# A decoder layer on one core: the heads' gate is projected ahead of the values, the values are turned round later, two exponentials are joined, and the first products of a block inverse run over 64 columns

## The chip, the core and the metric

The kernel runs on one core of a Trainium2 chip. The core has a matrix engine (TensorE, in the profile PE, with its weight loads in rows of their own, PEld), a vector engine (VectorE, DVE), an engine for activation functions (ScalarE, ACT), a general one (GpSimd, POOL) and one that here only starts transfers (SyncE, SP). The metric is the time of one execution on the device, in microseconds (us); the time before is the median of three runs, 2674.58 us.

## The reference, cut to what matters

One layer: a projection of 2048 tokens feeds four heads of a gated delta rule and four heads of HGRN2; their outputs go through an output projection, then come an MLP and a gated embedding. The change lies in the delta rule's heads (and one constant of the output projection's stage). Per head, with chunks of tokens:

```python
qkv = jax.nn.silu(causal_depthwise_conv(qkv, gdn_conv))      # four taps along time
q, k = l2norm(q), l2norm(k)
beta = jax.nn.sigmoid(b_gdn)
g    = -jnp.exp(a_log) * jax.nn.softplus(a_gdn + dt_bias)
gc   = jnp.cumsum(g, axis=-1)                                # inside a chunk
decay = jnp.exp(where(causal, gc[..., :, None] - gc[..., None, :], -inf))
lmat = einsum('bhncd,bhnsd->bhncs', k * beta[..., None], k) * decay
a_mat = eye(c) + where(strict, lmat, 0.0)                    # unit lower triangle
u = solve(a_mat, v * beta[..., None])
w = solve(a_mat, k * beta[..., None] * jnp.exp(gc)[..., None])
k_tail = k * jnp.exp(gc[..., -1:] - gc)[..., None]
# per chunk: v_new = u - w s ;  o = (q exp(gc)) s + qk v_new ;  s = s * exp(gc_last) + k_tail' v_new
o = gated_head_norm(o, gdn_norm, z_gdn)                      # rms norm, then times silu(z)
```

All of it is float32, with a tolerance that the kernel keeps by splitting the operands of its large products into two parts of a shorter float format.

## The kernel before, in words

**Stages.** The program runs through (1) the first embedding tiles, (2) the mixers: the input projection and the eight heads, one quarter `q` of 512 tokens after the other, (3) the output projection, (4) the MLP, (5) the gate of the embedding. The change touches stage 2, and one table of stage 3.

**The clock of stage 2.** For a quarter, `works` holds one small projection (`ab`, the decays) and then, for each of four head pairs `h`, eight projections of 128 channels in the order of `KINDS`: keys `k`, queries `q`, values `v`, the delta head's gate `z`, and HGRN2's `f`, `i`, query and gate. Their tiles are called `mm_4_q_h` (keys), `mm_0` (queries), `mm_8` (values), `mm_12` (the gate z), `mm_16`, `mm_20`, `mm_24`, `mm_28`. Each is 24 matmuls of 128 x 512 (three terms for each of eight slices of the model width) in three steps of eight; after each step a clock ticks (`tick`). A work's result is drained by its function (`to_k`, `to_z` and so on) after its third step. The PSUM banks of these projections come from a pool of two (`pm`), so that a projection cannot start before the one two places ahead has been drained. The first quarter also splits each weight tile on ACT and DVE (L172, L173) and stores the pair; the other quarters load the stored pair.

**A conv and a gate.** `conv_silu` (L557 on) drains a projection with one ACT copy (L560) and three DVE operations that read the bank (L564), one tick later comes the SiLU on ACT. A gate (`gate`, L597) is a single SiLU on ACT (L599).

**A delta head.** `gdn_mixer` is a generator; each of its steps is put into an agenda at a tick (`A_STEPS`, `A_FIRST` for the first head, `A_LAST` for the last, the first two steps of later heads by `A_AHEAD`). Counted from the start of its head's eight projections: the decays' exponentials (L637 to L647) at tick -6, the keys turned (`t_kg`) at 7, the products `kk` of keys with keys and queries at 10, the values turned (`t_vg`, L692, evacuated by four ACT copies into `vt`) and the triangle stored to DRAM (`ud`, L700) at 12, the triangle's 32 x 32 blocks solved by substitution on DVE (L719 to L735) at 16 to 23, the blocks joined to 64 and then to 128 by matmuls (`psp5`, `psx5`, `pst5`, then `psp6`, `psd6`, all by `pairs`, L753) at 30 to 36, and the four chunks' recurrence (`psa`, `psb`, `psc`) at 38 to 53. A head starts every 24 ticks, so the joining of one head's blocks lies beside the next head's keys, queries and values. The small matmuls are in float32 and use one pool of four banks (`pp`) in turn.

**What sets the order.** On PE and SP the instructions stand as the program writes them. On ACT and DVE a scheduler sets the order at build time. An engine runs its own queue strictly in order. An activation function that is not among those loaded is preceded by a load of a function table (`ACT_TABLE_LOAD`).

**Stage 3.** The output projection's tiles are computed in an order written out in `OUT_ORDER`; the norm of quarter 1's rows (`normed`) runs in steps at the ticks of `OUT_LAST` after its last tile: the sum of squares is split (`hl_o`), and at the second entry two matmuls with ones (`nrm_o`, L1197 and L1198) spread it.

## Time and profile before

| | |
|---|---|
| three runs | 2675.51, 2670.68, 2674.58 us |
| the profiled execution | 2671.73 us, of it 2669.9 us from the first instruction to the last |
| PE, PEld busy | 2639.4 us (99%), 2210.5 us (83%) |
| DVE, ACT, POOL busy | 1963.1 us (74%), 1491.8 us (56%), 136.4 us (5%) |
| granted clock of PE | 0.999 |
| transfers | 573.51 MB, 64% of the 16 engines' time on the main queue |

In the rows, a line number with a name is an operation's place in the kernel and the tile that it writes, with buffer numbers left out; `out<-in`, the shape, a count, and after the bar the busy time, the mean duration in ns and the idle time before it with what ended it. A float32 matmul of the program is two MATMUL records and two LDWEIGHTS records in the trace, a transpose one of each.

### The profile page before, as it was taken

To read this page: it belongs to the slowest core of one execution; us is meant where nothing else is said; L and a number is where in the kernel's file an instruction comes from. 1 tells how busy PE (TensorE), PEld (TensorE's weight loads), DVE (VectorE), ACT (ScalarE), POOL (GpSimd) and SP (SyncE) were. 2 spreads that over 40 slices of the span, in tenths; PEclk is the share of its full clock that TensorE was granted. 3 is DMA by queue.
4 is the path that set the end of the run, shared out by engine and by line. 5 is a ranking of instruction groups with operands and counts; after the bars stand their busy time and mean duration, and the time that the engine had idled before them with its cause. 6 is when DMAs were issued, how large, how long until landed. Compare 5 with 4: busy or idle time off the path is not lost. (4 is left out here: it accounts for less than half of the span.)

```text
span 2669.9 us, 38295 instructions
## 1 busy us (share of the span) xinstructions
PE 2639.4 (99%) x12745; PEld 2210.5 (83%) x12745; DVE 1963.1 (74%) x4016; ACT 1491.8 (56%) x3025; POOL 136.4 (5%) x147
## 2 busy tenths in 40 slices
PE   8899999999999999999999999999999999999999
PEld 6788888888888888878888888888888888888887
DVE  7677767777677677578988867767877765468776
ACT  7776655466546556566556555555555555565422
POOL 0000000000000000010000000001000001101000
PEclk9999999999999999999999999999999999999999
DMA  8777777667666665683665576666544465687663
GB/s 279 278 239 248 246 252 248 230 230 252 218 208 224 226 218 187 197 248 107 222 219 198 175 243 218 208 208 214 197 170 144 164 230 190 195 254 251 207 220 131
DMA packets 267766, 573.51 MB, mean 215 GB/s; under 512 B 55578, under 2 KB 60152, under 8 KB 250416
## 3 DMA queue, kind: packets, MB, share of 16 engines
q1 hardware_dynamic: 265264, 566.86, 64.0%
q0 software_dynamic: 2304, 4.20, 0.9%
q8 instruction: 101, 1.65, 0.3%
q14 instruction: 97, 0.79, 0.1%
HBM read 410.57 MB, written 160.37 MB: 214 GB/s over the span
## 5 line engine op out<-in xcount | busy, mean ns | idle before, releaser
L1134 PE MATMUL mm<-xt,w 128*128 128x512 f32 x3072 | 783.8, 400 | 5.4 <-DVE acc_vg L564 3.1
L1134 PEld LDWEIGHTS mm<-xt,w 128*128 128x128 f32 x3072 | 553.1, 189 | 106.4 <-issue 3.7
L1166 PE MATMUL d<-db,da 128*128 128x512 f32 x2688 | 612.8, 389 | 0.0
L1166 PE MATMUL u<-t,wu 128*128 128x512 f32 x2604 | 591.8, 389 | 0.1
L1166 PEld LDWEIGHTS d<-db,da 128*128 128x128 f32 x2688 | 504.5, 188 | 104.8
L1166 PEld LDWEIGHTS u<-t,wu 128*128 128x128 f32 x2604 | 488.6, 188 | 102.3 <-ACT wu L172 0.5
L226 DVE TENSOR_TENSOR db<-db 128x512 fp32r<-128x512 f32 x224 | 159.5, 712 | 59.5 <-ACT db L225 59.1
L1564 DVE TENSOR_TENSOR u<-u,u 128x512 f32<-128x512 f32 x224 | 150.4, 682 | 53.5 <-PE u L1166 52.0
L225 ACT ACTIVATE db<-db 128x512 fp32r<-128x512 f32 x224 | 140.9, 629 | 63.9 <-DMA db<-hid 61.4
L1166 PE MATMUL mmg<-h2T,wg 128*128 128x512 f32 (+1 forms) x792 | 174.7, 383 | 0.0
L1166 PEld LDWEIGHTS mmg<-h2T,wg 128*128 128x128 f32 x792 | 145.5, 188 | 29.1
L1607 ACT ACTIVATE u<-u 128x512 f32<-128x512 f32 x128 | 80.7, 630 | 154.2 <-DVE u L1564 153.8
L173 DVE TENSOR_TENSOR da<-da 128x512 fp32r<-128x512 f32 x128 | 94.2, 736 | 92.1 <-ACT da L172 91.7
L172 ACT ACTIVATE da<-da 128x512 fp32r<-128x512 f32 x128 | 80.6, 630 | 128.1 <-DMA da<-sumd 109.0
L1166 PE MATMUL mmo<-mixT,w_out 128*128 128x512 f32 x600 | 137.9, 390 | 1.7 <-DVE w_out L173 1.0
L1166 PEld LDWEIGHTS mmo<-mixT,w_out 128*128 128x128 f32 x600 | 112.4, 188 | 26.2 <-DVE w_out L173 1.9
L172 ACT ACTIVATE wu<-a 128x512 fp32r<-128x512 f32 x124 | 75.1, 623 | 53.0 <-DMA a<-in_w_up_dram 50.7
L173 DVE TENSOR_TENSOR wu<-a,wu 128x512 fp32r<-128x512 f32 x124 | 86.0, 695 | 8.8 <-ACT wu L172 8.3
L173 DVE TENSOR_TENSOR da<-dr,da 128x512 fp32r<-128x512 f32 x96 | 68.3, 711 | 25.6 <-ACT da L172 24.4
L1608 ACT ACTIVATE u<-u 128x512 f32<-128x512 f32 x128 | 80.4, 628 | 3.0
L172 ACT ACTIVATE da<-dr 128x512 fp32r<-128x512 f32 x96 | 60.5, 630 | 34.0 <-DMA dr<-in_w_down_dram 26.8
L242 POOL TENSOR_TENSOR acc_y<-acc_y,sq_y 128x512 f32<-128x512 f32 x28 | 38.1, 1359 | 757.7 <-ACT sq_y L241 757.7
(393 smaller groups left out, 3838.9 us busy)
## 6 DMA issues: line engine op xcount, KB each, us to landing
w<-cache_in SPq DMA_DIRECT2D x96, 1024.0 KB
db<-hid SPq DMA_DIRECT2D x224, 256.0 KB
cache_in<-w SPq DMA_DIRECT2D x32, 1024.0 KB
hid<-u SPq DMA_DIRECT2D x128, 256.0 KB
da<-sumd SPq DMA_DIRECT2D x128, 256.0 KB
a<-in_w_up_dram SPq DMA_DIRECT2D x124, 256.0 KB
hid<-ht SPq DMA_DIRECT2D x96, 256.0 KB
dr<-in_w_down_dram SPq DMA_DIRECT2D x96, 256.0 KB
```

The costliest lines, as they stand in the source:

```text
L172: S.activation(t[:, 0], raw, AF.Copy)
L173: eng.tensor_tensor(t[:, 1], raw, t[:, 0], ALU.subtract)
L225: S.activation(t[:, 0], plain(t), AF.Copy)
L226: V.tensor_tensor(t[:, 1], plain(t), t[:, 0], ALU.subtract)
L242: eng.tensor_tensor(acc, acc, sq, ALU.add)
L1134: PE.matmul(ps, *terms[i], start=i == 0, stop=i == nt - 1)
L1166: PE.matmul(ps, a, b, start=start, stop=stop)
L1564: V.tensor_tensor(c[new], c[old], ps, ALU.add)
L1607: S.activation(c[k], c[k], AF.Relu)
L1608: S.activation(c[k], c[k], AF.Square)
```

## The change

- `KINDS` projects the gate z third and the values fourth.
- The values' transposes and their four ACT copies move from the step at tick 12 into the first step of the substitution, at tick 16.
- `exp(gc)` (`eg`) was an ACT operation of its own into a tile `cc`; now DVE copies `gc` beside the tail's argument, and one ACT exponential takes both (128 x 8 for two of 128 x 4).
- `gb`, the tile of the decays' sums, is one tile zeroed once; before, each quarter zeroed it.
- The first joining of blocks multiplies only the 64 of 128 columns that are read afterwards: the right-hand operands of `psp5`, `psx5` and `pst5` are 64 columns wide, their left-hand operands stay 128 wide.
- `OUT_LAST` puts all steps after the first one tick later.

```diff
@@ -48,7 +48,7 @@
 SHARE = 6
 TOGETHER = ((1, 7), (1, 6))
 OUT_STEPS = (1, 5) + tuple(range(7, 20)) + (29, 31)
-OUT_LAST = (1, 4) + tuple(range(5, 18)) + (19, 23)
+OUT_LAST = (1, 5) + tuple(range(6, 19)) + (20, 24)
 MLP_STEPS = (1, 7) + tuple(range(9, 27, 2))
 AMID_STEPS = (1, 7) + tuple(range(12, 39, 3))
 
@@ -512,13 +512,14 @@
 
             return ready
 
+        gb = mt("gb", "gb", 1, (36, QT))
+        V.memset(gb, 0.0)
+
         def decays(ps, q):
 
-            gb = mt(f"gb_{q}", "gb", 1, (36, QT))
             sp = m2.tile([4, QT], F32, tag="tmp", name=f"sp_{q}")
             se = m2.tile([4, QT], F32, tag="th", name=f"se_{q}")
             S.activation(sp, ps[0:4, :], AF.Identity, bias=dec[:, 1:2])
-            V.memset(gb, 0.0)
             S.activation(gb[32:36, :], ps[32:36, :], AF.Tanh, scale=0.5)
             V.tensor_scalar(gb[32:36, :], gb[32:36, :], 0.5, 0.5, ALU.mult, ALU.add)
             V.scalar_tensor_tensor(se, sp, -1.0, sp, ALU.mult, ALU.max)
@@ -632,14 +633,14 @@
             gc = gcol[:, :, h : h + 1].rearrange("p c o -> p (c o)")
             beta = gcol[:, :, 32 + h : 33 + h].rearrange("p c o -> p (c o)")
             cd = sm.tile([P, NC], F32, tag="cd", name=f"cd_{n}")
-            tail = sm.tile([P, NC], F32, tag="tail", name=f"tail_{n}")
+            both = sm.tile([P, 2, NC], F32, tag="tail", name=f"tail_{n}")
+            tail, eg = both[:, 0], both[:, 1]
             glast = gf[:, :, P - 1]
             S.activation(cd, glast, AF.Exp)
             V.tensor_tensor(tail, glast, gc, ALU.subtract)
-            S.activation(tail, tail, AF.Exp)
-            both_cc = sm.tile([P, 2, NC], F32, tag="cc", name=f"cc_{n}")
-            eg, ncc = both_cc[:, 0], both_cc[:, 1]
-            S.activation(eg, gc, AF.Exp)
+            V.tensor_copy(eg, gc)
+            S.activation(both, both, AF.Exp)
+            ncc = sm.tile([P, NC], F32, tag="cc", name=f"cc_{n}")
             e = mt(f"e_{n}", "e")
             V.tensor_tensor(by_pair(e), by_pair(gf), negm[:, None].broadcast_to([P, NC // 2, 2, P]), ALU.add)
             for c in range(NC):
@@ -689,11 +690,6 @@
             V.tensor_tensor(qT, qT, flat(gf), ALU.mult)
             qg = qT
             yield
-            psv = turned(live.pop("v"), f"v{n}", pp)
-            vt = mt(f"vt_{n}", "vt", 2)
-            for c in range(NC):
-                S.activation(vt[:, c, :], psv[:, blk(c)], AF.Copy, scale=inv[:, c : c + 1])
-
             ud = dr.tile([NC, NB, SB, SB], F32, name=f"ud_{n}")
             for b in range(NB):
                 sl = slice(b * SB, (b + 1) * SB)
@@ -727,6 +723,10 @@
                 t = fix[:, :, :width]
                 V.tensor_tensor(t, below[:, part_m, part_i], next_to[:, part_m].broadcast_to([P, SB // 4, width]), ALU.mult)
                 V.tensor_tensor(above[:, part_m, part_i], above[:, part_m, part_i], t, ALU.add)
+            psv = turned(live.pop("v"), f"v{n}", pp)
+            vt = mt(f"vt_{n}", "vt", 2)
+            for c in range(NC):
+                S.activation(vt[:, c, :], psv[:, blk(c)], AF.Copy, scale=inv[:, c : c + 1])
             for i in range(0, SB, 2):
                 j = SB - 2 - i
                 if i:
@@ -760,20 +760,25 @@
 
 
 
-            psp = pair_bank("psp5")
-            pairs(psp, um[5], two(xn))
+            def ends(t):
+                return bass.AP(t.tensor, t.offset, [list(t.ap[0]), [P, 2], [3 * SB, 2], [1, SB]])
+
+            def half_bank(name):
+                return bank(f"{name}_{n}", pp)[:, : QT // 4].rearrange("p (a i) -> p a i", a=2)
+
+            psp = half_bank("psp5")
+            pairs(psp, um[5], ends(xn))
             for g in range(NB):
-                S.activation(part[5][rows_of(g), :, rows_of(g ^ 1)], psp[rows_of(g), :, rows_of(0 if g % 2 else 3)],
+                S.activation(part[5][rows_of(g), :, rows_of(g ^ 1)], psp[rows_of(g), :, rows_of(0 if g % 2 else 1)],
                              AF.Copy)
             yield
-            psx, pst = pair_bank("psx5"), pair_bank("pst5")
-            pairs(psx, two(xt), part[5])
-            pairs(pst, part[5], two(xt))
+            psx, pst = half_bank("psx5"), half_bank("pst5")
+            pairs(psx, two(xt), ends(part[5]))
+            pairs(pst, part[5], two(xt)[:, :, SB : 3 * SB])
             for g, to in ((1, 0), (2, 1)):
-                V.tensor_copy(by_pair(xn)[rows_of(g), :, g // 2, rows_of(to)], psx[rows_of(g), :, rows_of(3 * to)])
+                V.tensor_copy(by_pair(xn)[rows_of(g), :, g // 2, rows_of(to)], psx[rows_of(g), :, rows_of(to)])
             for g in range(NB):
-                at_b = rows_of(1 + g % 2)
-                S.activation(two(xt)[rows_of(g), :, at_b], pst[rows_of(g), :, at_b], AF.Copy)
+                S.activation(two(xt)[rows_of(g), :, rows_of(1 + g % 2)], pst[rows_of(g), :, rows_of(g % 2)], AF.Copy)
             yield
             psp = pair_bank("psp6")
             pairs(psp, um[6], two(xn))
@@ -964,7 +969,7 @@
         def to_hg(ps, q, h, g, b):
             b["z"] = gate(ps, f"gh{q}_{h}")
 
-        KINDS = ((4, to_k), (0, to_q), (8, to_v), (12, to_z), (16, to_f), (20, to_i), (24, to_hq), (28, to_hg))
+        KINDS = ((4, to_k), (0, to_q), (12, to_z), (8, to_v), (16, to_f), (20, to_i), (24, to_hq), (28, to_hg))
         decay = {}
         works = []```

**Where instructions stand, first place.** On DVE in the first quarter's first head: the products `kk` are multiplied by the decays (`u`, `qk`, `y_qg`), weights are split (`w_20`), and the values' taps `acc_vg` drain the bank of `mm_8`. Before:

```order
L685 TENSOR_SCALAR u_g0_0_898<-kk_g0_0_0_900,cc_g0_0_816,e_g0_0_818 128x128 x2
L688 TENSOR_TENSOR qk_g0_0_899<-kk_g0_0_0_900,e_g0_0_818 128x256
L564 TENSOR_SCALAR acc_vg0_0_860<-mm_8_0_0_784,cols_87,acc_vg0_0_860 128x509
L685 TENSOR_SCALAR u_g0_0_898<-kk_g0_0_2_908,cc_g0_0_816,e_g0_0_818 128x128
L564 TENSOR_SCALAR acc_vg0_0_860<-mm_8_0_0_784,cols_87,acc_vg0_0_860 128x510
L685 TENSOR_SCALAR u_g0_0_898<-kk_g0_0_2_908,cc_g0_0_816,e_g0_0_818 128x128
L564 TENSOR_SCALAR acc_vg0_0_860<-mm_8_0_0_784,cols_87,acc_vg0_0_860 128x511
L173 TENSOR_TENSOR w_20_0_0_868<-raw_20_0_0_780,w_20_0_0_868 128x1024
```

The same place after:

```order
L686 TENSOR_SCALAR u_g0_0_892<-kk_g0_0_0_894,cc_g0_0_817,e_g0_0_818 128x128 x2
L689 TENSOR_TENSOR qk_g0_0_893<-kk_g0_0_0_894,e_g0_0_818 128x256
L686 TENSOR_SCALAR u_g0_0_892<-kk_g0_0_2_902,cc_g0_0_817,e_g0_0_818 128x128 x2
L689 TENSOR_TENSOR qk_g0_0_893<-kk_g0_0_2_902,e_g0_0_818 128x256
L173 TENSOR_TENSOR w_20_0_0_862<-raw_20_0_0_780,w_20_0_0_862 128x1024
L690 TENSOR_TENSOR y_qg0_0_776<-y_qg0_0_776,gf_g0_0_737 128x512
L565 TENSOR_SCALAR acc_vg0_0_919<-mm_8_0_0_869,cols_87,acc_vg0_0_919 128x509
L565 TENSOR_SCALAR acc_vg0_0_919<-mm_8_0_0_869,cols_87,acc_vg0_0_919 128x510
L565 TENSOR_SCALAR acc_vg0_0_919<-mm_8_0_0_869,cols_87,acc_vg0_0_919 128x511
```

The values' taps stood between the operations on `kk`, and stand now behind all of them and behind a weight split.

**Second place.** On ACT at the end of the same head: `qk_h0_0` are the two halves of HGRN2's query SiLU that drain `mm_24`, `w_4_0_1` is the next head's first weight split, `cd`, `tail`, `e` and `gf` are the next head's decays. Before:

```order
L829 ACT_TABLE_LOAD
L829 ACTIVATE qk_h0_0_988<-mm_24_0_0_1052 128x256
L172 ACTIVATE w_4_0_1_1045<-raw_4_0_1_994 128x1024
L637 ACT_TABLE_LOAD
L637 ACTIVATE cd_g0_1_1065<-gf_g0_1_1028 128x4
L639 ACTIVATE tail_g0_1_1066<-tail_g0_1_1066 128x4
L646 ACTIVATE e_g0_1_1072<-e_g0_1_1072,gcol_0_800 128x128 x4
L647 ACTIVATE gf_g0_1_1028<-gf_g0_1_1028 128x512
L829 ACT_TABLE_LOAD
L829 ACTIVATE qk_h0_0_988<-mm_24_0_0_1052 128x256
```

After:

```order
L834 ACTIVATE iT_h0_0_1042<-mm_20_0_0_988 128x256 x2
L834 ACTIVATE qk_h0_0_978<-mm_24_0_0_1052 128x256 x2
L855 ACTIVATE hb_h0_0_1177<-qk_h0_0_978 128x256
L862 ACTIVATE hb_h0_0_1177<-qk_h0_0_978 128x256
L172 ACTIVATE w_4_0_1_1045<-raw_4_0_1_984 128x1024
L639 ACT_TABLE_LOAD
L639 ACTIVATE cd_g0_1_1065<-gf_g0_1_1028 128x4
L642 ACTIVATE tail_g0_1_1066<-tail_g0_1_1066 128x8
L647 ACTIVATE e_g0_1_1072<-e_g0_1_1072,gcol_0_800 128x128 x4
L648 ACTIVATE gf_g0_1_1028<-gf_g0_1_1028 128x512
```

The two halves now stand together, ahead of the decays and with one table load fewer; the next weight split stands behind two copies `hb` that need DVE's work on `qk_h`. Over the whole program ACT has 86 table loads before and 68 after.

**Third place.** On ACT in the second head, where the first head's blocks are joined: `part5` copies `psp5` and is read by `psx5` and `pst5`, `xt_g0_0` evacuates `pst5`, the `xs1` are sums of squares of the next quarter's input. Before:

```order
L660 ACTIVATE kt_g0_1_1324<-t_kg0_1_1319,tail_g0_1_1066 128x128 x4
L494 ACTIVATE xs1_0_1_1271,ss2_x1_1233<-xs1_0_1_1271 128x512
L766 ACTIVATE part5_577<-psp5_g0_0_1349 32x2x32 x4
L560 ACTIVATE acc_vg0_1_1369<-mm_8_0_1_1289,cols_87 128x512
L561 ACTIVATE hist_572<-mm_8_0_1_1289 128x3
L889 ACTIVATE keys_h0_0_4_1424<-qk_h0_0_988 128x2x4x32
L674 ACTIVATE q2_g0_1_1430<-y_qg0_1_1281 128x512
L172 ACTIVATE w_20_0_1_1377<-raw_20_0_1_1285 128x1024
L494 ACTIVATE xs1_1_0_1337,ss2_x1_1233<-xs1_1_0_1337 128x512
L776 ACTIVATE xt_g0_0_1201<-pst5_g0_0_1409 32x2x32 x4
```

After:

```order
L661 ACTIVATE kt_g0_1_1324<-t_kg0_1_1319,tail_g0_1_1066 128x128 x4
L574 ACTIVATE y_qg0_1_1281<-acc_qg0_1_1274 128x512
L772 ACTIVATE part5_577<-psp5_g0_0_1349 32x2x32 x4
L600 ACTIVATE zt_zg0_1_1369<-mm_12_0_1_1289 128x512
L894 ACTIVATE keys_h0_0_4_1418<-qk_h0_0_978 128x2x4x32
L675 ACTIVATE q2_g0_1_1424<-y_qg0_1_1281 128x512
L172 ACTIVATE w_16_0_1_1282<-raw_16_0_1_1220 128x1024
L494 ACTIVATE xs1_0_0_1234,ss2_x1_1233<-xs1_0_0_1234 128x512
L494 ACTIVATE xs1_0_1_1271,ss2_x1_1233<-xs1_0_1_1271 128x512
L781 ACTIVATE xt_g0_0_1201<-pst5_g0_0_1403 32x2x32 x4
```

The squares and a weight split moved from ahead of `part5` to between `part5` and `xt_g0_0`.

## The prediction

> **What bounds the kernel now.** I read the page first, then busy time by stretches (start and end, length, then busy time with counts of PE, PEld, DVE, ACT and POOL, PE's granted clock, the transfers' share), then PE's own waits (in all, times, longest).
>
> ```profile
> span 2669.9 us, 38295 instructions
> PE 2639.4 (99%) x12745; PEld 2210.5 (83%) x12745; DVE 1963.1 (74%) x4016; ACT 1491.8 (56%) x3025; POOL 136.4 (5%) x147
> 60.00:400.00 340.00, 331.81 (x1795) 282.51 (x1794) 252.35 (x690) 222.32 (x553) 17.84 (x21) 1.00 0.75 251
> 400.00:700.00 300.00, 299.20 (x1660) 257.84 (x1659) 222.88 (x650) 174.57 (x458) 19.41 (x22) 1.00 0.69 234
> 700.00:1060.00 360.00, 358.81 (x1987) 308.61 (x1986) 259.53 (x757) 197.36 (x513) 18.06 (x21) 1.00 0.68 218
> 1060.00:1250.00 190.00, 185.50 (x864) 153.72 (x863) 136.41 (x220) 115.65 (x200) 17.69 (x19) 1.00 0.65 197
> ```
>
> PE is the bound, at a granted clock of 1.00. It idles 30.5 us in all. In the stretches with the mixers (60 to 1060 us) it idles 8.2, 0.8 and 1.2 us, and 4.5 us in the one with the output projection. So the change can pay in two ways only: less work on PE, or fewer of these 14.7 us. What is saved on ACT or DVE alone is worth nothing where no row below waits for it.
>
> ```profile
> PE mm L1134 <- DVE acc_vg L564: 3.1, 1, 3.1
> PE nrm_o L1197 <- ACT hl_o L172: 2.6, 1, 2.6
> PE kk_g L681 <- ACT xt_g L776: 1.4, 1, 1.4
> PE mm L1134 <- ACT qk_h L829: 1.3, 1, 1.3
> PE kk_g L682 <- ACT y_qg L573: 0.7, 2, 0.4
> PE psx_g L753 <- ACT part L766: 0.7, 1, 0.7
> ```
>
> Five of the six lie in the first two heads, at 68 to 128 us. Each has a row in the steps below.
>
> **The 64 columns (PE work): taken as 0.** 16 heads x 6 matmuls (two each of `psp5`, `psx5`, `pst5`) x 2 records = 192 records get half the columns.
>
> ```profile
> 1062.02 0.60 PE L753 MATMUL psx_g<-part,xt_g 128*128 128x128 f32 x4
> 1062.46 0.61 PE L753 MATMUL pst_g<-xt_g,part 128*128 128x128 f32 x4
> L753 PEld LDWEIGHTS psx_g<-part,xt_g 128*128 128x128 f32 x64 | 9.6, 190 | 2.5 <-ACT part L766 1.1
> L594 PEld LDWEIGHTS t_vg<-cst,y_vg 128*128 128x128 f32 x64 | 7.6, 141 | 0.6
> 812.17 0.14 PEld L541 LDWEIGHTS ps_gb<-cst,gbb 36*128 36x128 f32 x1
> 812.24 0.14 PEld L541 LDWEIGHTS ps_gb<-cst,gb 36*128 36x128 f32 x1
> 812.48 0.30 PEld L1134 LDWEIGHTS mm<-xt,w 128*128 128x128 f32 x2
> ```
>
> Four records take 0.44 us from one start to the next group's, 0.11 us each. Is this the streaming of columns or the load of weights, which each record has? The last row is a pair of loads on an idle array, 0.30 us long with 0.19 for one: the second starts 0.11 us after the first, before the first matmul of 512 columns can have streamed. So a load of the 190-ns kind by itself holds the next one off for 0.11 us, what a record costs now. Loads for transposes are shorter (141 ns) and come 0.07 us apart with 36 columns behind them, so these rows don't bound ours from below. The weights stay 128 wide, so half the columns leave the 0.11 us. Bounds: nothing, or half of 192 x 0.11 = -10.6 us if streaming alone counts. I take nothing, since the load row is of the very shape. The Trainium skill ("TensorE: Matmul & The Clock Gate", Back-to-back issue gap) has the isolated gap go with the number of columns; by that rule the sum would get the full -10.6 us, a rival below. The same page's section on LDWEIGHTS gives 128 columns / 1.2, that is 107 ns, whatever the matmul behind it streams; by that the sum gets 0, and the 0.11 us of the pair of loads agrees.
>
> **The gate ahead of the values, first head: -2.7 us.** Before, three convolutions in a row need DVE, and the third shares it with `kk`.
>
> ```profile
> 71.99 0.61 DVE L685 SCALAR_TENSOR_TENSOR u_g<-kk_g,cc_g,e_g 128x128 f32<-128x128 f32 x2
> 72.52 0.41 DVE L688 TENSOR_TENSOR qk_g<-kk_g,e_g 128x256 f32<-128x256 f32 x1
> 73.39 1.04 ACT L172 ACTIVATE w<-raw 128x1024 fp32r<-128x1024 f32 x1
> 74.67 0.74 DVE L564 SCALAR_TENSOR_TENSOR acc_vg<-mm,cols,acc_vg 128x511 f32<-128x511 f32 x1
> 75.33 1.22 DVE L173 TENSOR_TENSOR w<-raw,w 128x1024 fp32r<-128x1024 f32 x1
> 75.56 2.06 PE L1134 MATMUL mm<-xt,w 128*128 128x512 f32 x8 [3.10 <-DVE acc_vg L564]
> 77.82 18.43 PE L1134 MATMUL mm<-xt,w 128*128 128x512 f32 x80
> ```
>
> PE could have gone on at 72.46 (75.56 less 3.10). After the change the bank that it needs then is the gate's, drained by one ACT operation; the values' bank is needed one projection later: 24 matmuls at 18.43/80 = 0.23 us, so at 72.46 + 5.5 = 78.0. On DVE (first order excerpt) come first four `u` and two `qk`, from 71.99 on 2 x 0.61 + 2 x 0.41 = 2.0, then the split (1.22, behind ACT's at about 73.2), `y_qg` (0.7, from the same timeline) and three taps (3 x 0.74): 71.99 + 2.0 + 1.2 + 0.7 + 2.2 = 78.1, with hand-overs 78.4. What is late next is this same bank, by 0.4. In later heads the same sum has no weight split, and about 1 us to spare.
>
> **Two halves of a SiLU together: -0.4 us.** Before, the second half stands behind the next head's decays and two table loads; after, it doesn't.
>
> ```profile
> 92.66 0.38 ACT L829 ACTIVATE qk_h<-mm 128x256 f32<-128x256 f32 x1 [3.48 <-PE mm L1134]
> 99.81 1.43 PE L1134 MATMUL mm<-xt,w 128*128 128x512 f32 x5 [1.27 <-ACT qk_h L829]
> 104.26 0.43 DVE L855 TENSOR_TENSOR qk_h<-qk_h,gg_h 128x256 f32<-128x256 f32 x1
> ```
>
> That wait (1.27) goes, but the second order excerpt puts the next weight split behind `hb`, which needs four DVE operations of 0.43 between pieces of the substitution. From the end of `mm_24`: two halves 0.7, DVE 4 x 0.43 + 0.75, `hb` 0.43, split 1.04 on ACT, decays' two DVE operations 0.85, split 1.22: 6.7 us, against 24 matmuls and four transposes on PE, 5.9. A wait of 0.8 to 0.9 takes its place.
>
> **The second head: -1.8 us.**
>
> ```profile
> 119.64 1.06 ACT L172 ACTIVATE w<-raw 128x1024 fp32r<-128x1024 f32 x1 [0.18 <-DMA cache_in<-w]
> 120.89 0.63 ACT L494 ACTIVATE xs<-xs 128x512 f32<-128x512 f32 x1 [0.19 <-DMA xs<-in_x_dram]
> 123.38 0.88 ACT L766 ACTIVATE part<-psp_g 32x64 f32<-32x64 f32 x4
> 124.31 0.71 PE L753 MATMUL psx_g<-part,xt_g 128*128 128x128 f32 x4 [0.72 <-ACT part L766]
> 127.31 0.89 ACT L776 ACTIVATE xt_g<-pst_g 32x64 f32<-32x64 f32 x4
> 128.25 0.49 PE L681 MATMUL kk_g<-y_kg 128*128 128x128 f32 x2 [1.44 <-ACT xt_g L776]
> ```
>
> The split and two squares (1.06, and 0.85 each with the read of the sum) leave the way to `part`: its 0.72 goes. They now lie ahead of `xt_g`: gate 0.6, keys 0.42, `q2` 0.63, split 1.06, squares 1.7 = 4.4 us behind `part` (the short ones from the same timeline). `part` then begins about 1.2 us after `psp5` starts, so `xt_g` ends at 1.2 + 0.9 + 4.4 + 0.9 = 7.4 us, where the third `kk` product comes at 7.0 to 7.2. Of 1.44 some 0.4 stays: -0.72 - 1.04.
>
> **Joined exponentials, `gb` once, and the other heads: -1.0 us.**
>
> ```profile
> L642 ACT ACT_TABLE_LOAD x13 | 16.7, 1283 | 0.2
> 60.25 0.48 DVE L521 MEMSET gb<- 36x512 f32 x1 [2.41 <-PE ps_gb L541]
> L639 ACT ACTIVATE tail_g<-tail_g 128x4 f32<-128x4 f32 x16 | 3.3, 203 | 5.6 <-DVE tail_g L638 5.5
> 70.03 0.17 DVE L663 COPY rk_g<-ssk_g 128x4 f32<-128x4 f32 x1
> ```
>
> 18 table loads fewer are 23 us of ACT, 16 exponentials of 0.2 another 3; DVE gets 16 copies of 0.17 and loses three zeroings, one of which held its queue 2.41 us at 60. All of it lies beside PE. It is worth what of the small waits stands behind ACT: idle 10.2 us from 60 to 1060 less the rows above (3.1, 1.44, 1.27, 0.72 and one of 0.4) is 3.2 us. I take a third off; bounds -3.2, and +3.2 if the moved transposes and copies bring as many small waits as they remove. The transposes themselves keep their number; at tick 16 they are followed by `psc` only, and their first reader is many ticks off.
>
> **The norm one tick later: -1.8 us.**
>
> ```profile
> 1163.69 0.50 PE L1197 MATMUL nrm_o<-hl_o,ones 128*128 128x512 f32 x1 [2.57 <-ACT hl_o L172]
> ```
>
> Eight matmuls (8 x 0.23 = 1.8) now fill 2.57 of waiting; bounds -2.6 (also the last of it) and 0. What follows from that norm starts 1.8 us later and has five tiles of matmuls ahead of it.
>
> **The sum.** -2.7 - 0.4 - 1.8 - 1.0 - 1.8 = -7.7 us. The profiled execution took 2671.73 us (1.8 around its span), so 2664.0; it is 2.85 under the median of the runs, from which the same sum gives 2666.9. I say 2666 us, -0.3%. Less than 0.2% (5.3 us) can't be told from no change here.
>
> **The rivals.**
> - *Streaming decides* (half the columns, half the record): -10.6 more, 2655 us. For it: 0.11 us is also what 128 float32 columns might stream in. Against: the pair of loads. 8%.
> - *The waits come back*: PE arrives 5 us earlier at places where transfers and ACT set the pace (a split waiting for `cache_in` in the row at 119.64), and only the norm and `part` keep their gain: -2.5, 2672 us. For it: the first quarter's heads are where ACT and DVE also split weights; against: DVE 74%, ACT 65% busy in that stretch. 25%.
> - *Slower: the values' bank becomes late in every head.* From `kk` to the projection that needs it PE has 1.8 + 1.8 + 5.5 + 0.9 = 10.0 us; the chain on DVE and ACT (`kk` 1.8, `u` and `qk` 1.1 behind it, ACT's copies 1.8 and `acc` 0.7, three taps 2.2, two other DVE pieces 1.1) takes 8.7 to 8.9. It decides from 1.2 us more of other work: a weight split and one more tap's worth of DVE (1.22 + 0.74 + 0.2) give 1 us per head, 16 in all: 2674.6 - 7.7 + 16 = 2683 us. For it: taps of the values already made PE's longest wait. Against: only the first quarter splits weights. 12%.
>
> **How the numbers follow.** The forecast (-5.3 to -11) has 55%, the rivals 8, 25 and 12. Faster by over 0.2%: 55 + 8 = 63%; within: 25%; slower: 12%. The range 2656 to 2673 us holds the forecast, the returned waits and the edge of the streaming case; the slower case is left out.
>
> **What would show it.** Rows of `psx_g` and `pst_g` at 128x64 with starts 0.11 us apart show the loads in charge, at 0.06 the streaming. The wait of `mm` for `acc_vg` should fall from 3.1 to about 0.4, for `part` vanish, for `hl_o` fall to about 0.75; idle PE time from 60 to 1060 us should fall from 10.2 to some 5 us. The forecast is wrong if `mm` waits for `acc_vg` in many heads, or if new rows as long as the old ones stand at the same places.

## The result, and the profile after

The changed kernel takes 2665.96 us (median of 9 runs, 2665.34 to 2671.68) where the kernel before takes 2672.27 us beside it (9 runs, 2667.45 to 2675.66): a ratio of 0.9981, 95% interval 0.9973 to 0.9990. The ratio is worked out from the single runs and is not quite that of the two medians (0.9976): by the ratio the change gains 5.1 us, by the medians 6.3. The profiled execution took 2665.86 us, its span is 2664.1 us. The prediction said 2666. A later measurement, beside its own runs of the kernel before, gave 2669.67 against 2674.64 us, a ratio of 0.9980 (0.9971 to 0.9989): the size holds, the absolute times don't carry over.

The page of the changed kernel, and its busy time by the stretches that the prediction read (start and end, length, then PE, PEld, DVE, ACT and POOL, the granted clock, the transfers' share, GB/s):

```profile
span 2664.1 us, 38284 instructions
PE 2637.0 (99%) x12745; PEld 2209.8 (83%) x12745; DVE 1968.0 (74%) x4029; ACT 1468.8 (55%) x2991; POOL 136.4 (5%) x147
```

```profile
60.00:400.00 340.00, 336.26 (x1823) 287.65 (x1824) 259.21 (x724) 215.03 (x548) 17.83 (x21) 1.00 0.77 259
400.00:700.00 300.00, 298.61 (x1656) 257.42 (x1655) 219.26 (x631) 165.70 (x447) 19.55 (x22) 1.00 0.68 229
700.00:1060.00 360.00, 358.81 (x1994) 309.35 (x1992) 264.03 (x766) 193.98 (x508) 18.14 (x21) 1.00 0.68 218
1060.00:1250.00 190.00, 186.20 (x852) 152.81 (x851) 136.50 (x217) 116.17 (x198) 17.66 (x19) 1.00 0.63 193
```

ACT lost 23.0 us (1491.8 to 1468.8), about what 18 table loads of 1.28 us come to. PE's idle time in the mixers fell from 10.2 to 3.7 + 1.4 + 1.2 = 6.3 us, all of it in the first stretch (8.2 to 3.7); the second rose from 0.8 to 1.4, and the third stands where it stood. Of PE's own waits in the changed kernel, those that bear on the change:

```profile
PE kk_g L683 <- ACT y_qg L574: 2.5, 3, 1.8
PE psc_g L810 <- ACT w_g L807: 1.1, 2, 0.7
PE u L1171 <- ACT w_u L172: 0.9, 1, 0.9
PE mm L1139 <- DVE w L173: 0.8, 1, 0.8
PE nrm_o L1202 <- ACT hl_o L172: 0.8, 1, 0.8
PE at_h L889 <- DVE acc_vg L566: 0.7, 1, 0.7
PE u L1171 <- DVE w_u L173: 0.4, 1, 0.4
```

The rows `mm <- acc_vg` (3.1), `mm <- qk_h` (1.3), `kk <- xt_g` (1.4) and `psx <- part` (0.7) are gone. New are 1.8 us of `kk` for the queries in the first head (0.4 before), a wait of `mm` for a split weight, two waits of the MLP's first tiles (`u`) for one, and one of HGRN2's `at_h` behind the values' taps; the recurrence's waits (`psc`) grew from 0.3 to 1.1.

A table worked out from the starts of matmuls in the traces shows where the span changed. The stages are: start to the first head's first `kk`; from there to the third head's; from there to the first matmul of the output projection; from there to the first of the embedding gate; the rest.

| kernel | to kk, 1st head | two heads | 14 heads | output projection and MLP | rest | span |
|---|---|---|---|---|---|---|
| before | 67.99 | 121.33 | 856.24 | 1444.97 | 179.42 | 2669.95 |
| changed | 67.71 | 116.19 | 856.30 | 1444.44 | 179.41 | 2664.06 |
| difference | -0.28 | -5.14 | +0.06 | -0.53 | -0.01 | -5.89 |

So 5.1 of 5.9 us were won in two of sixteen heads. Each row is one execution: the changed kernel's second profile, a_full below, has 115.58 and 859.38 in the third and fourth columns, so that a stage can differ by 3 us with nothing changed.

### The profile page after: what moved, and what is told of

It is laid out like the page before. It is cut to its first block, busy times and chain, and to the rows that moved or that the text cites. A ratio compares the mean times of both kernels' runs of the same rounds, so it can differ in the third digit from the quotient of the medians.

```text
span 2664.1 us, 38284 instructions
## 1 busy us (share of the span) xinstructions
PE 2637.0 (99%) x12745; PEld 2209.8 (83%) x12745; DVE 1968.0 (74%) x4029; ACT 1468.8 (55%) x2991; POOL 136.4 (5%) x147
## 4 chain that ended last, share of the span: by engine, by line
PE 60%; DMA 3%; DVE 2%; ACT 1%; issue 1%; SPq 0%; POOL 0%; DVEq 0%; ACTq 0%; POOLq 0%
PE d L1171 23%; PE u L1171 23%; PE mmg L1171 7%; PE mm L1139 3%; PE mmo L1022 1%; PE mme L199 1%; DMA mixT<-mixd 1%; DMA yod<-yo 1%; DMA yo<-in_xT_dram 0%; DVE t L173 0%; DVE acc_o L242 0%; DMA sys_g<-ud_g 0%; DMA wd<-in_w_down_dram 0%; PE at_h L889 0%; DMA ud_g<-u_g 0%
## 5 line engine op out<-in xcount | busy, mean ns | idle before, releaser
L1139 PE MATMUL mm<-xt,w 128*128 128x512 f32 x3072 | 783.6, 400 | 1.3 <-DVE w L173 0.8
L1139 PEld LDWEIGHTS mm<-xt,w 128*128 128x128 f32 x3072 | 553.3, 189 | 102.0 <-issue 1.3
L1171 PE MATMUL d<-db,da 128*128 128x512 f32 x2688 | 612.8, 389 | 0.0
L1171 PEld LDWEIGHTS d<-db,da 128*128 128x128 f32 x2688 | 504.5, 188 | 104.8
L1171 PE MATMUL u<-t,wu 128*128 128x512 f32 x2604 | 591.2, 389 | 0.0
L1171 PEld LDWEIGHTS u<-t,wu 128*128 128x128 f32 x2604 | 488.7, 188 | 101.5
L1171 PE MATMUL mmg<-h2T,wg 128*128 128x512 f32 (+1 forms) x792 | 174.7, 383 | 0.0
L1171 PEld LDWEIGHTS mmg<-h2T,wg 128*128 128x128 f32 x792 | 145.5, 188 | 29.1
L173 DVE TENSOR_TENSOR da<-da 128x512 fp32r<-128x512 f32 x128 | 95.4, 745 | 88.8 <-ACT da L172 85.5
L172 ACT ACTIVATE da<-da 128x512 fp32r<-128x512 f32 x128 | 80.5, 629 | 126.1 <-DMA da<-sumd 106.5
L1171 PE MATMUL mmo<-mixT,w_out 128*128 128x512 f32 x600 | 138.4, 390 | 1.5 <-DVE w_out L173 1.1
L1171 PEld LDWEIGHTS mmo<-mixT,w_out 128*128 128x128 f32 x600 | 112.2, 188 | 26.6 <-DVE w_out L173 2.3
L172 ACT ACTIVATE wu<-a 128x512 fp32r<-128x512 f32 x124 | 75.1, 624 | 54.6 <-DMA a<-in_w_up_dram 52.7
L173 DVE TENSOR_TENSOR wu<-a,wu 128x512 fp32r<-128x512 f32 x124 | 85.8, 694 | 9.3 <-ACT wu L172 9.1
L173 DVE TENSOR_TENSOR da<-dr,da 128x512 fp32r<-128x512 f32 x96 | 68.2, 710 | 22.9 <-ACT da L172 21.4
L172 ACT ACTIVATE da<-dr 128x512 fp32r<-128x512 f32 x96 | 60.5, 631 | 30.5 <-DMA dr<-in_w_down_dram 19.6
```

Of the source, the lines that this page charges most:

```text
L172: S.activation(t[:, 0], raw, AF.Copy)
L173: eng.tensor_tensor(t[:, 1], raw, t[:, 0], ALU.subtract)
L1139: PE.matmul(ps, *terms[i], start=i == 0, stop=i == nt - 1)
L1171: PE.matmul(ps, a, b, start=start, stop=stop)
```

## The experiments

All times are medians in us, beside those of the kernel before in the same session; a ratio is to its runs. The stages are those of the table above, of one profiled execution for each row. "Order" is the gate ahead of the values with the values' transposes moved; "cols" the 64 columns; "exps" the joined exponentials with the single zeroing; "norm" the steps one tick later.

| kernel | parts | time | before | ratio (95%) | two heads | 14 heads | output, MLP |
|---|---|---|---|---|---|---|---|
| e1_cols | cols | 2674.91 | 2673.09 | 1.0007 (0.9998 to 1.0016) | 120.39 | 858.08 | 1447.89 |
| e2_gate | order | 2669.63 | 2673.09 | 0.9990 (0.9981 to 0.9999) | 117.40 | 859.87 | 1446.75 |
| e3_exp | exps | 2671.83 | 2673.09 | 0.9998 (0.9989 to 1.0007) | 118.94 | 856.55 | 1446.19 |
| e4_last | norm | 2672.30 | 2673.09 | 1.0000 (0.9991 to 1.0009) | 120.24 | 857.05 | 1445.29 |
| e_vt | transposes alone | 2677.33 | 2674.59 | 1.0008 (0.9999 to 1.0017) | 121.45 | 860.10 | 1446.73 |
| gate_last | order, norm | 2670.90 | 2674.59 | 0.9989 (0.9980 to 0.9998) | 117.85 | 855.34 | 1448.37 |
| a_nogate | cols, exps, norm | 2673.22 | 2674.64 | 0.9993 (0.9984 to 1.0002) | 117.39 | 857.77 | 1445.00 |
| a_noexp | order, cols, norm | 2668.14 | 2674.64 | 0.9973 (0.9964 to 0.9983) | 116.06 | 856.70 | 1447.31 |
| a_noexp2 | the same | 2669.11 | 2674.59 | 0.9980 (0.9971 to 0.9989) | 115.42 | 857.73 | 1447.82 |
| a_full | all | 2669.67 | 2674.64 | 0.9980 (0.9971 to 0.9989) | 115.58 | 859.38 | 1444.57 |
| a_late8 | all, first exps later | 2669.56 | 2674.64 | 0.9980 (0.9971 to 0.9989) | 115.50 | 856.44 | 1448.82 |

### The 64 columns alone

```diff
-            psp = pair_bank("psp5")
-            pairs(psp, um[5], two(xn))
+            psp = half_bank("psp5")
+            pairs(psp, um[5], ends(xn))
...
-            pairs(psx, two(xt), part[5])
-            pairs(pst, part[5], two(xt))
+            pairs(psx, two(xt), ends(part[5]))
+            pairs(pst, part[5], two(xt)[:, :, SB : 3 * SB])
```

> The kernel before with the 64 columns alone. Theory (the load of 128 weights sets the pace): the records of psp5, psx5 and pst5 keep starts 0.11 us apart, PE's busy time stays at 2639 us, the time within 1 us of before. Rival (the streaming of columns sets it): starts 0.055 us apart and -10.6 us.

The time did not fall: 1.0007, +1.9 us (-0.5 to +4.3), where the theory allowed 1 and streaming asked for -10.6. The changed kernel's rows (start, length) say why; four records of `pst` at 64 columns still take 0.44 us to the next group (for `psx` it is 0.39, and the records of `at_h` behind take 0.05 longer to the next projection):

```profile
1056.42 0.55 PE L753 MATMUL psx_g<-part,xt_g 128*128 128x64 f32 x4
1056.81 0.61 PE L753 MATMUL pst_g<-xt_g,part 128*128 128x64 f32 x4
1057.25 0.66 PE L889 MATMUL at_h<-qk_h,keys_h 128*128 128x128 f32 x4
```

Between two records of such a group lie 0.11 us. From the projection matmul ahead of `psx`, `pst` and `at_h` to the one behind them it is 1.49 us (median of starts over the heads) before, after, and with this part alone. But the edit is not without effect: in the second head the waits for `part` and `xt_g` are gone in this kernel, though no instruction outside these three products and the copies out of their banks differs. On ACT, in time order, with this part alone:

```profile
122.52 0.89 ACT L772 ACTIVATE part<-psp_g 32x64 f32<-32x64 f32 x4
124.89 0.89 ACT L781 ACTIVATE xt_g<-pst_g 32x64 f32<-32x64 f32 x4
125.81 0.42 ACT L792 ACTIVATE xt_full<-xt_g 64x256 f32<-64x256 f32 x1
126.13 1.04 ACT L172 ACTIVATE w<-raw 128x1024 fp32r<-128x1024 f32 x1
```

Here a weight split stands behind `xt_g` and `xt_full`; before, it ran at 125.75, ahead of them. Compared through the whole trace, DVE's order differs from before in 170 pieces and ACT's in 79. The scheduler that writes these two engines' order at build time wrote another one, because three products of a third engine got narrower. What that is worth beside the new order of the projections shows further down, in gate_last against a_noexp.

### What a float32 record costs

To the changed kernel, behind `psp5` in the second quarter's four heads, thirty matmuls each whose results nobody reads:

```diff
+                for i in range(6):
+                    PE.matmul(spare[:, :P], w5[:, i % 2], x5[:, i % 2], start=True, stop=True)
+                for i in range(6):
+                    PE.matmul(spare[:, :SB], w5[:, i % 2], x5[:, i % 2, :SB], start=True, stop=True)
+                for i in range(6):
+                    PE.matmul(spare[:64, :P], w5[:, i % 2, :64], x5[:, i % 2], start=True, stop=True)
...
```

> The changed kernel with thirty more float32 matmuls behind psp5 in each of the second quarter's four heads, whose results nobody reads: six each with weights of 128 columns and 128 and 32 columns of data, of 64 columns with 128 and 64, and of 32 with 32. Theory (a record costs the longer of its load of weights and its streaming): starts 0.11 us apart at 128 x 128, 128 x 32 and 64 x 128, half of that at 64 x 64, a quarter or a floor above it at 32 x 32. Rival (the load costs the same whatever its width): 0.11 us in all five. Second rival (streaming sets it): 0.03 us at 128 x 32.

One head's five groups of twelve records each, in time order:

```profile
365.19 1.56 PE L775 MATMUL psp_g<-xn_g,um 128*128 128x128 f32 x12
366.59 1.42 PE L777 MATMUL psp_g<-xn_g,um 128*128 128x32 f32 x12
367.94 1.52 PE L779 MATMUL psp_g<-xn_g,um 128*64 128x128 f32 x12
369.30 0.86 PE L781 MATMUL psp_g<-xn_g,um 128*64 128x64 f32 x12
370.09 0.56 PE L783 MATMUL psp_g<-xn_g,um 128*32 128x32 f32 x12
```

The medians of the starts' distance, over 44 pairs each: 112 ns (weights of 128 columns, 128 of data), 112 (128, 32), 109 (64, 128), 58 (64, 64), 32 ns (32, 32). So a record costs the longer of the two: a quarter of the data alone saves nothing, and half the weights alone 3 ns. Per column it is 0.85 to 0.91 ns down to 64. That is the theory as put; at 32 x 32 it is 32 ns, 4 over a quarter. The 14 heads took 879.80 us in this kernel's one execution, 20.4 and 23.5 more than in the two profiles of the changed kernel; 48 records at each of the five prices come to 20.3. The Trainium skill ("TensorE: Matmul & The Clock Gate", LDWEIGHTS) has a load take its columns over 1.2 in ns, so 107, 53 and 27 for 128, 64 and 32; where the data is no wider than the weights, the trace's distances lie some 5 ns above these.

### The order of the projections, with the transposes moved

```diff
-        KINDS = ((4, to_k), (0, to_q), (8, to_v), (12, to_z), (16, to_f), (20, to_i), (24, to_hq), (28, to_hg))
+        KINDS = ((4, to_k), (0, to_q), (12, to_z), (8, to_v), (16, to_f), (20, to_i), (24, to_hq), (28, to_hg))
...
-            psv = turned(live.pop("v"), f"v{n}", pp)
...
+            psv = turned(live.pop("v"), f"v{n}", pp)
             for i in range(0, SB, 2):
```

> The kernel before with the gate ahead of the values and the values' transposes in the substitution, nothing else. Theory (most of the gain is the order of the projections): the rows mm <- acc_vg 3.1, mm <- qk_h 1.3, kk <- xt_g 1.4 and psx <- part 0.7 go, a wait of mm for a split weight of 0.8 comes; PE's idle time falls by 3 to 5 us from 60 to 1060 us; kk <- y_qg of the first head stays at 0.44. Time -3 to -5 us. Rival (the gain is ACT's relief by the table loads): under -1 us here, since ACT's table loads stay.

The ratio is 0.9990: 2.7 us, just under the 3 to 5 that were expected, and well over the rival's 1. The rows behaved much as the theory said: all four are gone, two waits for a split weight came (0.52 and 0.97, where one of 0.8 was expected), and the first two heads are 3.9 us shorter. But the later heads gave 3.6 us back in this execution, so that PE's idle time from 60 to 1060 us fell by 0.7 us only, not by 3 to 5. The longest of it, on PE and then on DVE:

```profile
466.04 0.46 PE L799 MATMUL psb_g<-r_g,xt_full 128*128 128x128 f32 x2 [2.59 <-DVE r_g L796]
```

```profile
464.67 0.17 DVE L638 TENSOR_TENSOR tail_g<-gf_g,gcol 128x4 f32<-128x4 f32 x1 [3.54 <-DMA gf_g<-gd]
464.75 0.69 DVE L644 TENSOR_TENSOR e_g<-gf_g,cst 128x512 f32<-128x512 f32 x1
465.55 0.34 DVE L796 SCALAR_TENSOR_TENSOR r_g<-psa_g,cc_g,vt_g 128x128 f32<-128x128 f32 x1
```

DVE stood 3.54 us before the decays of the next head, whose transfer had not landed, and what PE needed stood behind them in the queue. No other profile shows a wait of PE of over 0.35 us within 20 us of it.

### The transposes' place alone

```diff
-            psv = turned(live.pop("v"), f"v{n}", pp)
...
+            psv = turned(live.pop("v"), f"v{n}", pp)
             for i in range(0, SB, 2):
```

> The kernel before with the values' transposes moved into the substitution and the order of the projections left. Theory (the order is the gain, the transposes' place is worth nothing): the wait of mm for acc_vg of 3.1 us stays or grows into one of its neighbours, second head's kk within 1 us of before, time within 2 us of before. Rival (four transposes and four ACT copies fewer between kk and the values' bank are what frees it): mm <- acc_vg falls under 1.5 us and the time by 2 to 3 us.

The wait stands, to the hundredth:

```profile
76.08 4.18 PE L1133 MATMUL mm<-xt,w 128*128 128x512 f32 x9 [3.10 <-DVE acc_vg L564]
```

The ratio is 1.0008 (-0.3 to +4.5 us): 2.1 us more, and the second head's `kk` comes 1.2 us later than before, both just over what the theory allowed, neither a gain. The order is all that this kernel and the one above differ in, so it is the order of the projections that removes this wait. The wait of 3.10 us also stands unmoved with the columns alone and with the norm's steps alone. The rows of the second head are not so tied to the order: here the wait of `mm` for `qk_h` is down to 0.50, and that of `kk` is 0.76, for another tile.

### The joined exponentials alone

```diff
-            S.activation(tail, tail, AF.Exp)
-            both_cc = sm.tile([P, 2, NC], F32, tag="cc", name=f"cc_{n}")
-            eg, ncc = both_cc[:, 0], both_cc[:, 1]
-            S.activation(eg, gc, AF.Exp)
+            V.tensor_copy(eg, gc)
+            S.activation(both, both, AF.Exp)
+            ncc = sm.tile([P, NC], F32, tag="cc", name=f"cc_{n}")
...
-            V.memset(gb, 0.0)
```

> The kernel before with the joined exponentials and the tile of the decays' sums zeroed once, nothing else. Theory: ACT's busy time falls by 23 us or so, and PE gains nothing of it: what the small waits lose (0 to -1 us) is given back in the first head, where kk's wait for y_qg grows from 0.44 to about 1.8, since the load of the exponentials' table no longer falls into the time in which ACT waits for a stored weight. Net 0 to +1.5 us. Rival (ACT's relief is the gain): -3 us, the waits for acc_vg, qk_h and xt_g shrink here too. Second rival for the new wait: it belongs to the gate's order, then it is at 0.44 here.

ACT's busy time fell by 24.1 us (1491.8 to 1467.7) and the time by nothing that can be told: 0.9998, -2.9 to +1.9 us. The rival was not wholly wrong, though: the waits for `acc_vg`, `qk_h` and `xt_g` are gone here too, and the two heads are 2.4 us shorter. But where 3.10 us of `acc_vg` stood, there are now 1.21 of `mm` for the gate's SiLU and 1.79 of the transposes for `y_vg`, 3.0 in all; a_nogate below, which also joins the exponentials and keeps the old order, has 2.39 and 0.60 there, 3.0 again. Only in the kernels with the order is it 0.6 or less. The 1.8 us that the theory expected at `kk` did not come: no wait for `y_qg` over 0.35 us stands in this first head.

### The norm's steps alone

```diff
-OUT_LAST = (1, 4) + tuple(range(5, 18)) + (19, 23)
+OUT_LAST = (1, 5) + tuple(range(6, 19)) + (20, 24)
```

> The kernel before with the norm's steps one tick later, nothing else. Theory: the wait of nrm_o for hl_o falls from 2.57 to about 0.75, -1.8 us; the waits of u for w_u at the start of the MLP (0.9 and 0.4 in the changed kernel) come with it, so that -0.5 to -1.8 us stays. Rival: those waits belong to something else and are not here; then the whole -1.8 us.

PE's waits in this kernel:

```profile
PE u L1166 <- ACT w_u L172: 0.9, 1, 0.9
PE nrm_o L1197 <- ACT hl_o L172: 0.5, 1, 0.5
PE u L1166 <- DVE w_u L173: 0.4, 1, 0.4
```

The norm's wait fell from 2.57 to 0.5, and the MLP's two waits came with it, as the theory said. They stand in the eight profiles with the new steps that the tables list and in none of the five that have the old ones (the kernel before among these). The ninth with the new steps, the kernel with thirty more matmuls, has neither; there PE had waited 2.28 us for an output weight some 20 us ahead. The ratio is 1.0000, and the time of the stage shows no gain either: 1444.4 to 1448.8 us with the new steps (mean of eight 1446.5), 1445.0 to 1447.9 with the old (mean of five 1446.5).

### The change without the joined exponentials, and without the order

> The changed kernel with the exponentials apart and the tile of the decays' sums zeroed per quarter, as before: 64 columns, the order of the projections and the norm's steps are those of the change. Theory (the parts add up): kk's wait for y_qg in the first head is at 0.4, the second head's kk comes 3.6 us earlier than in the kernel before, the norm gives 1.6 us, -4 to -5.5 us against before. Rival (the gain of the order lasts only where ACT is relieved of 23 us): the early gain is lost again between the third and the tenth head, -1 to -2 us against before.

> The changed kernel with the old order of the projections and the values' transposes at their old place; 64 columns, joined exponentials and the norm's steps are those of the change. Theory: the second head's kk comes 2.2 us earlier than before (as with the joined exponentials alone), the norm gives 1.6 us less what u then waits for w_u, -2 to -3 us against before. Rival (the order of the projections does nothing that the joined exponentials don't do): -5 us, as the whole change.

Without the exponentials the gain is as large or larger (0.9973, which is 7.2 us where 4 to 5.5 were expected, then 0.9980, table above); without the order it is 0.9993, 1.9 us, not told from none. Of seven measurements with the order (of five kernels) every one is at 0.9990 or under, of five without it every one is at 0.9993 or over. The later heads kept their length in the first (856.70, before 856.24), so the rival that the early gain needs ACT's relief falls. The parts do not add up in the first two heads: these take 117.39 us in a_nogate, without the order, and 117.40 in e2_gate, with the order alone, since several of the parts remove the same waits.

> The changed kernel without the joined exponentials and the single zeroing, once more. Theory (the relief of ACT is worth nothing, and the -7.2 us of the first time are the gain of -5 us and chance): -4.5 to -7 us. Rival (joining the exponentials costs time): -7 us or more again, 2 us under the changed kernel.

The repeat lies between: -5.3 us, inside the interval of the first and the same as the whole change. That joining the exponentials costs time is not shown, nor that it brings any: the whole change and this kernel are at the same 0.9980, with intervals of 2.4 us to either side, in which a gain or loss of 1 us would not show.

> The kernel before with the gate's order, the values' moved transposes and the norm's steps; neither the 64 columns nor the joined exponentials. Theory (these two parts are the gain, the others nothing): -5 to -7 us against before, second head's kk 3.6 us earlier. Rival (the 64 columns were part of the gain of -7 us): -3 us as with the gate's order alone.

0.9989, -2.9 us: the rival's number, and the second head's `kk` comes 2.8 us earlier, not 3.6. a_noexp adds the 64 columns to this kernel and nothing else, and its two measurements (0.9973 and 0.9980) are 2.4 to 4.3 us lower, though the intervals overlap and the columns alone gave +1.9. PE's price of the products is not behind it (section on the columns). The order that the scheduler writes on DVE is, for a part that the traces show. With the order and without the columns, in this kernel (first two lines) and in e2_gate, a split for a norm stands behind a weight split; with the columns (a_noexp, last two lines) it stands ahead:

```profile
157.95 1.21 DVE L173 TENSOR_TENSOR w<-raw,w 128x1024 fp32r<-128x1024 f32 x1
159.69 0.68 DVE L173 TENSOR_TENSOR hl_h<-osq_h,hl_h 128x512 fp32r<-128x512 f32 x1
155.49 0.69 DVE L173 TENSOR_TENSOR hl_h<-osq_h,hl_h 128x512 fp32r<-128x512 f32 x1
156.37 1.23 DVE L173 TENSOR_TENSOR w<-raw,w 128x1024 fp32r<-128x1024 f32 x1
```

PE's `nrm_h` waits 0.96 and 0.97 us for that split in the two without the columns, and not at all in the six profiles that have the order and the columns. Their first two heads take 115.1 to 116.2 us, against 117.4 and 117.9. So beside the new order the narrower products are worth some 2 us in these heads, by the order of another engine, and this wait is half of it; whether the rest of the totals' difference is more than chance stays open.

### The changed kernel once more, and the first head's new wait

> The changed kernel as it is, once more, beside the others of this call. Theory (the waits that the trace shows are made by the build's order of work, not by this one execution): kk <- y_qg 1.84 in the first head, mm <- w 0.8, nrm_o <- hl_o 0.8 and u <- w_u 0.9 and 0.4 come again within 0.3 us, and the time is 5 us under before. Rival (a single execution's late transfers make much of it): two or more of these rows are gone or others of over 1 us stand in 135 to 1060 us, and the gain is under 3 us.

The gain came again (-5.3 us). Of the rows, `mm <- w` (0.73) and `u <- w_u` (0.89 and 0.41) did within 0.3 us, and `nrm_o <- hl_o` did with 0.5 more (1.34); `kk <- y_qg` in the first head did not (0.25), and `psp <- xn` of 1.25 and `at_h <- acc_vg` of 1.71 us stand in the later heads, where the 14 heads took 3.1 us more than in the first execution. So theory and rival each hold in part.

Why was the first head's wait of 1.84 us there once? On ACT the table load for the exponentials stands at another place. The changed kernel, first execution:

```profile
63.58 1.06 ACT L172 ACTIVATE w<-raw 128x1024 fp32r<-128x1024 f32 x1 [2.59 <-DMA cache_in<-w]
64.66 1.28 ACT L639 ACT_TABLE_LOAD   x1
67.96 1.28 ACT L574 ACT_TABLE_LOAD   x1
69.26 0.63 ACT L574 ACTIVATE y_qg<-acc_qg 128x512 f32<-128x512 f32 x1
```

With the exponentials apart (a_noexp):

```profile
60.93 1.28 ACT L642 ACT_TABLE_LOAD   x1
62.49 1.04 ACT L172 ACTIVATE w<-raw 128x1024 fp32r<-128x1024 f32 x1
67.80 0.63 ACT L573 ACTIVATE y_qg<-acc_qg 128x512 f32<-128x512 f32 x1
```

The small exponential that was taken away needed only the columns of sums, so its table load stood ahead of a weight split; without it the load stands behind the split, which waits for a store of an earlier one (`cache_in`). The queries' SiLU comes 1.46 us later (69.26 against 67.80). But the new order alone does not make the wait. In a_full, the same kernel, the split waits 0.68 us:

```profile
62.94 1.06 ACT L172 ACTIVATE w<-raw 128x1024 fp32r<-128x1024 f32 x1 [0.68 <-DMA cache_in<-w]
```

It waits 0.83 to 0.89 in the three other profiles with the joined exponentials at this place, and 2.59 in the first execution alone. From the start of `hist`, which ends the draining of the queries' bank on ACT, to the start of their SiLU it is 6.8 us in those four, 8.4 in the first execution, and 7.0 to 7.1 in all kernels with the exponentials apart; PE's wait for the queries is 0.14 to 0.25 in those four, 1.84 in the first execution, and 0.41 to 0.45 with the exponentials apart. So the wait of 1.84 us was one late transfer, and the new order by itself is 0.2 us shorter than the old.

> The changed kernel with the first head's exponentials one tick later, so that its SiLU of the queries stands ahead of them on ACT and needs no second load of a table. Theory (the new wait of 1.84 us is this order on ACT alone): kk's wait for y_qg in the first head falls to under 0.1 and the second head's kk comes 1.8 us earlier, -1.8 us against the changed kernel. Rival (the exponentials are then late for the products behind kk): the wait comes back as one of mm for acc_vg or of psp for xn, and nothing is won.

```diff
-A_FIRST = (3, 7, 8, 8, 9, 10, 12, 14) + tuple(range(16, 24)) + (24, 26, 29, 32, 34, 36, 37)
+A_FIRST = (3, 8, 8, 8, 9, 10, 12, 14) + tuple(range(16, 24)) + (24, 26, 29, 32, 34, 36, 37)
```

No wait for `y_qg` stands in its first head, a short one for the gate's SiLU came (0.39), and the time is that of the changed kernel (2669.56 against 2669.67). The two heads are as long as in a_full (115.50 and 115.58). The gain of 1.8 us is not there, since the wait was not there in the execution beside it either. At 1144 us PE lost 2 us, where ACT in this kernel waits for an output weight:

```profile
1142.87 1.06 ACT L172 ACTIVATE w_out<-raw_out 128x1024 fp32r<-128x1024 f32 x1 [1.37 <-DMA raw_out<-in_w_out_dram]
```

PE waits 2.13 us for that split; in the first execution of the changed kernel ACT made it at 1140.39, and PE waited 0.78 at that place, for DVE's part of it. No version was found that is faster than the changed kernel by more than the intervals.

## Why the prediction was right, point by point

The sign came out, and the time: 2666 against 2665.96. That the time did to the tenth is luck. The forecast was 7.7 us under the kernel before; measured beside it the gain is 5.1 us by the ratio (an interval of 2.7 to 7.2) or 6.3 by the medians, and the kernel before stood 2.3 us lower in these runs than in the three that the forecast started from. In the later measurement the changed kernel is at 2669.67. By the ratio the gain is even just short of the 5.3 at which the forecast itself set the bound of what can be told; the interval holds both sides. The terms of the order of the projections come to -4.9 in the first two heads, where the profiles have -5.1; but with the order and without the columns (e2_gate, gate_last) it is -3.9 and -3.5, so that the agreement is in part luck as well; the norm and the joined exponentials, -2.8 together, brought -0.5 in these profiles. PE's idle time from 60 to 1060 us fell to 6.3 us, where some 5 were expected (6.7 in a_full).

- **The 64 columns, 0: right** for PE's work, and the rival that streaming decides is out, by the starts 0.11 us apart, by the ratio 1.0007 and by the five widths. What the term left out is that the edit rewrites ACT's and DVE's order: beside the new order of the projections that is worth some 2 us in the first two heads.
- **The gate ahead of the values, -2.7: right.** The wait for `acc_vg` fell from 3.10 to nothing that PE's rows show in the changed kernel, and to 0.54 and 0.50 in a_noexp and gate_last, where 0.4 was worked out. The transposes alone leave it at 3.10.
- **Two halves of a SiLU together, -0.4: right.** 1.27 became 0.81 for the next split, as forecast (0.8 to 0.9); it is 0.73 to 1.02 in every other kernel with the order. In three of these (e2_gate, gate_last, a_late8) a second wait of 0.41 to 0.52 for a split stands 7 us ahead of it, and nothing is won.
- **The second head, -1.8: right in size, a little small.** Both waits went whole (0.72 and 1.44); of the 0.4 that was to stay, a_full shows 0.30, for `xn` of the same step. But both are gone with the columns alone and with the exponentials alone too, so the way that the term works out is one of several by which they go.
- **Joined exponentials and the other heads, -1.0: not borne out.** The reason given was that a third of the small waits stands behind ACT. The mixers' idle time less the rows named for other steps and less the late transfer of the first head is 6.3 - 0.8 - 1.8 = 3.7 us where it was 3.2, so these waits did not become fewer; the 14 later heads took 856.30 for 856.24 us. In time it can't be told: ACT's relief alone gave 0.9998, whose interval of -2.9 to +1.9 us holds the -1.0. The bounds of the term held it.
- **The norm, -1.8: a third of it at most.** The wait fell to 0.81, where 0.75 was worked out; the sentence that what follows "has five tiles of matmuls ahead of it" is what failed, since the MLP's first tiles then waited 0.87 + 0.41 = 1.28 us. The stage kept -0.5, and over all profiles nothing that shows. Why the splits of those tiles come later was not traced.

A size was missing throughout. A removed wait is worth more than its row. The MLP's second product in the kernel before (count, shortest, median and longest ns of one):

```profile
L1166 PE MATMUL d<-db,da x2688: 389/389/389, 1552.6 to 2490.3; 128*128 128x512 f32 x192
```

A matmul's modelled length is 0.39 us where the next starts 0.23 after it, and idle time is counted from that end. So each wait that vanishes gives 0.16 more; with three fewer in two heads this is some 0.5 us (an estimate) of the 5.1, which the rows alone (6.5 gone; 0.8 come, and 1.4 more at `y_qg`) put at 4.3. The rest, 0.3, was not traced further.

Of the rivals, *the waits come back* held in single places: `w_u` in the MLP, and late transfers in the first head of one execution, at 464 us in e2_gate and at 1143 us in a_late8. The first two heads kept their gain. *The values' bank late in every head* did not come as a wait of `mm`; a relative of it did, in the rows of `at_h`. On DVE, in a_full:

```profile
895.45 0.69 DVE L1096 TENSOR_TENSOR wd<-wd,wd 128x512 f32<-128x512 f32 x1 [1.86 <-DMA wd<-in_w_down_dram]
896.05 0.74 DVE L565 SCALAR_TENSOR_TENSOR acc_vg<-mm,cols,acc_vg 128x511 f32<-128x511 f32 x1
896.72 0.41 DVE L895 TENSOR_TENSOR qk_h<-qk_h,gg_h 128x256 f32<-128x256 f32 x1
897.05 0.15 DVE L566 TENSOR_TENSOR acc_vg<-acc_vg,bound 128x3 f32<-128x3 f32 x1
```

The last tap of the values stands behind an operation that waits for a transfer, and behind the tap the `qk_h` that `at_h` reads; the row names `acc_vg`, whose last piece ended last. It is 0.7 and 1.7 us in the two executions of the changed kernel, in one head, not sixteen.

## What to carry to other kernels

Order the work so that the bank that PE needs next is drained by one operation of an engine that is free by then, not by three of a busy one: exchanging two projections gave 2.7 us by itself, 23 us less of ACT's busy time nothing that can be told. A float32 product is made cheaper by narrowing weights and data together, since a record costs the longer of the two. And where a scheduler writes the order of two engines, cost an edit by the order that the build gives and by several executions, since a part that is worth nothing by itself moves waits elsewhere, and late transfers make waits of 1 to 2.6 us in one execution that the next does not have.

## What the runs showed of the hardware that was not expected

The clock at the start differs from execution to execution. In the kernel before PE pauses for 2.28 us up to 19.22:

```profile
19.22 6.16 PE L199 MATMUL mme<-pT,w_plea 128*128 128x512 f32 x18 [2.28 <-ACT pT L172]
```

The changed kernel has the same pause (2.27). In the 2 us behind it, the kernel before and then the changed kernel (the last three numbers are the granted clock, the transfers' share, GB/s):

```profile
20.00:22.00 2.00, 1.99 (x6) 1.58 (x6) 1.78 (x3) 0.72 (x2) 0.00 (x0) 0.50 0.88 163
```

```profile
20.00:22.00 2.00, 1.95 (x8) 1.61 (x9) 1.80 (x3) 1.23 (x3) 0.00 (x0) 1.00 0.89 126
```

The projection begins at 40.17 us in the first and at 39.21 in the second; in a_full, the same kernel as the second with a clock of 0.94 over its first 60 us, at 41.14. So the 1 us between the two kernels at that point need not be the change's; by the first `kk` 0.28 of it is left. The Trainium skill ("TensorE: Matmul & The Clock Gate", Part 1: The HAM clock gate) has a window of 3.4 us that runs freely, so that the same kernel meets it in another phase each time; the halved clock in one execution of a kernel and not in the other agrees (from 22 to 24 us 0.50 in a_full, 1.00 in the first execution), while the pauses here, 2.3 us and 1.7 in a_full, are shorter than that window.
